# Gathering the small experts in pairs, and moving a transposition, in a two-layer decoder kernel

## The chip, the cores and the metric

One core of a Trainium2 chip runs the whole kernel in one launch. The metric is device time in microseconds (us): the median of three runs, 1362.1 us before the change (1359.48 to 1362.96). Lower is better. The profile is of a single execution of the same kernel.

## The reference

Two post-LayerNorm decoder layers on 256 tokens of width 1024, all in float32. Layer 0 mixes (pooling and window attention) and applies a dense SwiGLU; layer 1 mixes (dilated attention and a short convolution) and applies a SwiGLU of 8 experts, of which each token takes 2. The change lies in those experts, whose computation is, cut to its core:

```python
logits = xt @ w_router
top_logit, top_e = lax.top_k(logits, 2)
gates = jax.nn.softmax(top_logit, axis=-1)
# for each expert e, on the tokens that chose it:
y = (jax.nn.silu(xb @ w_gate[e]) * (xb @ w_up[e])) @ w_down[e]
# added back to each token, times its gate
x = layer_norm(ALPHA * x + out)
```

An expert's weights are 1024 x 3584 for gate and for up and 3584 x 1024 for down. All of them are read, whatever the routing.

## The kernel before

Weights come in pieces of 128 x 2048 float32 (1 MB), one DMA each in the expert stage, issued by SP in the order of use as soon as one of the raw buffers is free. A float32 product is made from rounded halves (fp32r): ScalarE casts a piece to its high half (`wh`, `hi()`, L258), VectorE subtracts that from the raw piece for the low half (`wl`, `lo()`, L275), and TensorE multiplies with both. Four wh and three wl buffers run in rings. Each time TensorE is done with a piece (`drop`), `pump` issues the next cast and, at most two pieces ahead, the next subtraction. A few pieces are "native": TensorE multiplies the raw float32 piece without a split.

Each engine works through its instructions in the order of the program, which is written out by hand (`manual_schedule`).

The experts are sorted by their number of tokens. If at least five of seven have 64 tokens or fewer, these five are "light" (1 to 5), the others (0, 6, 7) "heavy"; this is the branch that runs here. An expert has 7 chunks of 512 inner columns; a chunk is one call of `step`: gate (two pieces), up (two pieces), then the two down products of the chunk before it (`prev`), since its activations have to be turned in between. The order of chunks (`mixed`) interleaves light and heavy ones, mostly one heavy, two light.

- A heavy chunk has tokens in high and low halves, 128 columns each, and each product takes three matmuls (`mm3`, L316 to L318). Its down pieces are native in most of the run (L1224). ScalarE applies silu to the gate, VectorE multiplies with up (L1441), TensorE transposes the result (L1246).
- A light chunk packs high and low halves of up to 64 tokens as 128 columns, so two matmuls do (L1226, L1227). TensorE transposes gate (`fold_of` into `sg`, L1237), ScalarE copies one half of the result (L1240), VectorE adds the other (L1241, the sg sum), ScalarE applies silu (L1436). Up is copied out (L1439), transposed and summed the same way into `us`; the transposes and the copy stand between the two down products, the us sum and the product sg x us (L1466) behind both.

Before an expert starts, its tokens are gathered by matmuls with a one-hot matrix `oh` (VectorE, L1169): `half` (L1185) or `thin` (L1190), products in L1179, with the tokens' high and low halves `xkh` and `xkl` as separate fp32r products. These halves are made once, by `copy` and `tensor_sub` at L1089, L1091, L1115 and L1306. `part()`, called after gate and after up of every step, runs the next part of a gather that is queued; `part(p)` at the start of a step finishes that of p. `follow` queues the next gather. Light gathers go to the two halves of `places[1]`, heavy ones to `places[0]`.

Of the kernel before, what the change touches and what calls it, by code (L numbers as in the profile page):

```python
# [10 lines left out]
F32 = mybir.dt.float32  # L11
F32R = mybir.dt.float32r
# [8 lines left out]
KC = D // 128  # L21
# [66 lines left out]
def trunk(ctx, tc, stream, x_tok, x_t, pos, ln_w, ln_b, pool_bd, pool_sc, sinks, conv_w, router, cf, cb, windows,  # L88
# [798 lines left out]
    with tc.tile_pool(name="od1", bufs=1) as e1, tc.tile_pool(name="od2", bufs=2) as e2:  # L887
# [153 lines left out]
    raw3 = ctx.enter_context(tc.tile_pool(name="raw3", bufs=1))  # L1041
    xk, yb = [raw2.tile([128, PIECE], F32R, name=f"xk{i}") for i in range(2)], \
        raw2.tile([128, PIECE], F32R, name="yb")
    raws = [raw3.tile([128, PIECE], F32, name=f"raw{RAW1 + i}") for i in range(RAW2 + RAW3 - 3)]
# [3 lines left out]
    ctx.enter_context(tc.manual_schedule())  # L1048
    xkh, xkl = [t.rearrange("p (i d) -> p i d", i=2) for t in xk]
    lgp = bank()  # L1050
    lg0 = lgp[:, :2 * NE].rearrange("p (i e) -> p i e", e=NE)

    def route(norm, c):
# [10 lines left out]
        return logits  # L1064

    def split_tokens(i):
        split(xkh[:, i], xkl[:, i], x[:, i])

# [19 lines left out]
    lga = route(na, 4)  # L1088
    nc.scalar.copy(xkh[:, 0], x[:, 0])  # L1089
    lgb()  # L1090
    nc.vector.tensor_sub(xkl[:, 0], x[:, 0], xkh[:, 0].bitcast(F32))  # L1091
    lgb = route(na, 6)
# [21 lines left out]
    keep(KEEP[2])  # L1114
    nc.scalar.copy(xkh[:, 1], x[:, 1])  # L1115
    W.hi()
# [44 lines left out]
    class Unit:  # L1161
# [13 lines left out]

        def gather(self, a, c, b, m):
            for k in range(c, c + 512 // m):
                for i in range(2):
                    nc.tensor.matmul(b[:, (k - c) * m:(k - c + 1) * m],  # L1179
                                     (xkh, xkl)[a][:, i, k * 128:(k + 1) * 128],  # L1180
                                     self.oh[:, i], start=i == 0, stop=i == 1)

        def half(self, c, a, b, copy):
            self.gather(a, c, b, 128)
            copy(self.xg[a][:, c:c + 4], b.rearrange("p (k s) -> p k s", s=128))  # L1185

        def thin(self, a):
            b = bank()
            self.gather(a, 0, b, LIGHT)
            nc.scalar.copy(self.xg[0][:, :, a * LIGHT:(a + 1) * LIGHT], b.rearrange("p (k s) -> p k s", s=LIGHT))  # L1190

        def parts(self):
            yield self.start()
            for j in range(2 if self.light else 4):
                if self.light:
                    self.thin(j)
                else:
                    self.half(4 * (j % 2), j // 2, bank(), nc.vector.tensor_copy if j == 3 else nc.scalar.copy)
                yield

# [90 lines left out]
    m2 = ctx.enter_context(tc.tile_pool(name="mo2", bufs=1, side="right"))  # L1291
    rings.add("oh", [m2.tile([128, 2, 128], F32R, name="oh")])
    rings.add("ohb", [m2.tile([128, 2, 128], F32R, name="ohb")])
# [8 lines left out]
    rings.add("bank", [bank() for _ in range(4)])  # L1302
    places = [big_tile(t) for t in ("mh", "ml")]
    unit = Unit(places[0], 0, False, slot)
    unit.start()
    nc.vector.tensor_sub(xkl[:, 1], x[:, 1], xkh[:, 1].bitcast(F32))  # L1306
    W.lo()
    for c in (0, 4):
        unit.half(c, 0, acc(), nc.scalar.copy)
    for c in (0, 4):  # L1310
        unit.half(c, 1, bank(), nc.vector.tensor_copy if c == 0 else nc.scalar.copy)
    for _ in range(4):
# [6 lines left out]
    def gates():  # L1319
        nc.vector.tensor_scalar(gt[:, 0], gt[:, 1], 1.0, None, op0=OP.add)  # L1320
        nc.vector.reciprocal(gt[:, 0], gt[:, 0])
        nc.vector.tensor_mul(gt[:, 1], gt[:, 1], gt[:, 0])
        nc.vector.tensor_mul(gate, hots[0], bc(gt[:, 0]))
        nc.vector.tensor_mul(hots[1], hots[1], bc(gt[:, 1]))
        nc.vector.tensor_add(gate, gate, hots[1])
        nc.scalar.activation(x, x, AF.Copy, scale=ALPHA)

# [41 lines left out]
    class Experts:  # L1369
# [14 lines left out]
        def gather(self, p):  # L1384
            light = p in self.light
            half = KC * 128
            place = places[1][:, p % 2 * half:(p % 2 + 1) * half] if light else places[self.kind(p)]
            self.units[p] = Unit(place, p, light, slots)
            self.queue.append((p, self.units[p].parts()))

# [16 lines left out]
        def step(self, s):  # L1407
# [37 lines left out]
            if self.prev is not None:  # L1445
# [4 lines left out]
                W.drop()  # L1450
            if light:
                fold_up = fold_of(us, h)
            if left == 0:
                unit.back()
            if self.prev is not None:
                finish(down_half(self.y[pe], pht, 1, pn, W.take(None)))
                W.drop()
                if ended:
                    split_y(yb[:, :D], yb[:, D:], self.y.pop(pe))
                    ended.back()  # L1460
                    self.todo = combine_of(pe, ended.oht)
            if light:
                ht = rings.next("hh")
                s3 = sg.rearrange("p (k t) -> p k t", t=LIGHT)
# [20 lines left out]
        def follow(self, p, n):  # L1485
            if not self.light:
                after = p + 1 if n == 1 and p else None
            elif p in self.light:
                after = p + 1 if n == 0 and p + 1 in self.light else None
            else:  # L1490
                after = next((q for q in range(p + 1, NE) if q not in self.light), None) if n == NCH - 1 else None
# [15 lines left out]
    def tail(x8):  # L1507
# [4 lines left out]
        for _ in range(7):  # L1512
            nc.tensor.matmul(spare, xkh[:, 0, :128], xkh[:, 0, :512], start=True, stop=True)
        e, n, ht = x8.prev
# [207 lines left out]
```

## Time and profile before

| | |
|---|---|
| median of three runs | 1362.1 us |
| the profiled execution | 1365.56 us |
| its span, first to last instruction | 1363.8 us |
| TensorE busy | 1321.2 us, 97% |
| VectorE busy | 1084.4 us, 80% |
| ScalarE busy | 917.3 us, 67% |
| granted TensorE clock, mean | 0.990 |
| the page's row of DMA, mean of the span | 313 GB/s |

The expert stage runs from about 470 us to 1345 us. Times of rows are us from the first instruction. Engines are PE (TensorE; PEld its weight loads), DVE (VectorE), ACT (ScalarE) and SP. A row of a timeline is one group of instructions: start, time from the first start to the last end, engine, line, operation, written tile <- read tiles, shape, count; in brackets is the idle time of the engine just before and what ended it. Matmuls overlap, and their ends are modelled, so the distance of two starts says more than the length of a row. A native product shows as two records.

### The profile page before, as it was taken

To read this page: it belongs to the slowest core of one execution; us is meant where nothing else is said; L and a number is where in the kernel's file an instruction comes from. 1 tells how busy PE (TensorE), PEld (TensorE's weight loads), DVE (VectorE), ACT (ScalarE), POOL (GpSimd) and SP (SyncE) were. 2 spreads that over 40 slices of the span, in tenths; PEclk is the share of its full clock that TensorE was granted. 3 is DMA by queue.
4 is the path that set the end of the run, shared out by engine and by line. 5 is a ranking of instruction groups with operands and counts; after the bars stand their busy time and mean duration, and the time that the engine had idled before them with its cause. 6 is when DMAs were issued, how large, how long until landed. Compare 5 with 4: busy or idle time off the path is not lost. (4 is left out here: it accounts for less than half of the span.)

```text
span 1363.8 us, 18760 instructions
## 1 busy us (share of the span) xinstructions
PE 1321.2 (97%) x6944; PEld 1069.5 (78%) x6944; DVE 1084.4 (80%) x1110; ACT 917.3 (67%) x1026; POOL 2.5 (0%) x8
## 2 busy tenths in 40 slices
PE   8999999999999989999999999999999999999995
PEld 6888999988999778877777777787777877777764
DVE  6866555587655688899898899898889979988987
ACT  5735444455544477788776788778678769776883
POOL 0000000000000000000000000000000000000000
PEclk9999999999999999999999999999999999999998
DMA  8617655535424689999999999999999999999991
GB/s 261 234 62 222 205 187 186 187 124 186 155 78 149 261 307 370 346 417 401 420 387 362 377 420 420 418 419 419 419 392 419 419 405 419 420 419 350 418 411 41
DMA packets 72375, 426.61 MB, mean 313 GB/s; under 512 B 8914, under 2 KB 9682, under 8 KB 30548
## 3 DMA queue, kind: packets, MB, share of 16 engines
q1 hardware_dynamic: 71412, 424.32, 79.9%
q0 software_dynamic: 576, 0.62, 0.3%
q8 instruction: 56, 0.92, 0.3%
q10 hardware_dynamic: 288, 0.39, 0.1%
q14 instruction: 43, 0.35, 0.1%
HBM read 424.88 MB, written 1.05 MB: 312 GB/s over the span
## 5 line engine op out<-in xcount | busy, mean ns | idle before, releaser
L275 DVE TENSOR_TENSOR wl<-raw,wh 128x2048 fp32r<-128x2048 f32 (+2 forms) x435 | 823.6, 1914 | 155.6 <-ACT wh L258 126.9
L258 ACT CAST wh<-raw 128x2048 fp32r<-128x2048 f32 (+2 forms) x437 | 695.0, 1607 | 140.1 <-PE bank L318 62.8
L1226 PE MATMUL bank<-wh,ml 128*128 128x512 f32 x536 | 220.5, 411 | 1.1 <-ACT h L1427 1.1
L1227 PE MATMUL bank<-wl,ml 128*128 128x512 f32 x536 | 211.5, 395 | 0.9 <-DVE wl L275 0.6
L318 PE MATMUL bank<-wl,mh 128*128 128x512 f32 x336 | 131.8, 392 | 3.1 <-DVE wl L275 3.1
L316 PE MATMUL bank<-wh,mh 128*128 128x512 f32 x336 | 134.0, 399 | 0.0
L317 PE MATMUL bank<-wh,mh 128*128 128x512 f32 x336 | 131.4, 391 | 0.4 <-ACT mh L1185 0.4
L1227 PEld LDWEIGHTS bank<-wl,ml 128*128 128x128 f32 x536 | 100.8, 188 | 28.5 <-DVE wl L275 6.1
L1226 PEld LDWEIGHTS bank<-wh,ml 128*128 128x128 f32 x536 | 100.8, 188 | 22.6 <-issue 3.1
L316 PE MATMUL bank<-xth,wh 128*128 128x256 f32 x416 | 118.1, 284 | 0.0
L317 PE MATMUL bank<-xth,wl 128*128 128x256 f32 x416 | 117.7, 283 | 0.0
L318 PE MATMUL bank<-xtl,wh 128*128 128x256 f32 x416 | 117.7, 283 | 0.0
L1226 PE MATMUL acc<-wh,hh 128*128 128x512 f32 (+1 forms) x308 | 115.3, 381 | 0.8 <-DVE hh L1468 0.8
L1224 PE MATMUL acc<-raw,hf 128*128 128x512 f32 x256 | 115.2, 593 | 0.0
L1227 PE MATMUL acc<-wl,hh 128*128 128x512 f32 (+1 forms) x308 | 112.9, 373 | 0.0
L1224 PEld LDWEIGHTS acc<-raw,hf 128*128 128x128 f32 x256 | 47.1, 190 | 47.1 <-issue 46.0
L316 PEld LDWEIGHTS bank<-xth,wh 128*128 128x128 f32 x416 | 79.8, 192 | 0.4
L317 PEld LDWEIGHTS bank<-xth,wl 128*128 128x128 f32 x416 | 79.8, 192 | 0.4
L318 PEld LDWEIGHTS bank<-xtl,wh 128*128 128x128 f32 x416 | 79.8, 192 | 0.0
L318 PEld LDWEIGHTS bank<-wl,mh 128*128 128x128 f32 x336 | 63.5, 189 | 16.9 <-DVE wl L275 3.5
L317 PEld LDWEIGHTS bank<-wh,mh 128*128 128x128 f32 x336 | 63.5, 189 | 14.6 <-issue 1.0
L316 PEld LDWEIGHTS bank<-wh,mh 128*128 128x128 f32 x336 | 63.5, 189 | 13.8 <-issue 1.0
(284 smaller groups left out, 1849.0 us busy)
## 6 DMA issues: line engine op xcount, KB each, us to landing
raw<-in_stream SPq DMA_DIRECT2D x326, 1024.0 KB, 9.8
raw<-in_stream SPq DMA_DIRECT2D x142, 512.0 KB, 4.9
ln_wb<-in_ln_w SPq DMA_DIRECT2D x3, 512.0 KB, 8.1
ln_wb<-in_ln_b SPq DMA_DIRECT2D x3, 512.0 KB, 9.5
xraw<-in_x_t SPq DMA_DIRECT2D x4, 256.0 KB, 7.2
raw<-in_stream SPq DMA_DIRECT2D x4, 256.0 KB, 5.0
x<-in_x_tok SPq DMA_DIRECT2D x1, 1024.0 KB, 7.0
win<-in_windows SPq DMA_DIRECT2D x1, 768.0 KB, 10.9
```

Source lines behind the costliest of these rows:

```text
L258: nc.scalar.copy(self.split[k][0][:, c], self.raw[k][:, c])
L275: nc.vector.tensor_sub(wl[:, c], self.raw[k][:, c], wh[:, c].bitcast(F32))
L316: nc.tensor.matmul(o, ah, bh, start=start, stop=False)
L317: nc.tensor.matmul(o, al, bh, start=False, stop=False)
L318: nc.tensor.matmul(o, ah, bl, start=False, stop=stop)
L1224: nc.tensor.matmul(o, a if a.dtype == F32 else a.bitcast(F32), bh, start=start, stop=stop)
L1226: nc.tensor.matmul(o, a, bh, start=start, stop=False)
L1227: nc.tensor.matmul(o, a, bl, start=False, stop=stop)
```

## The change

The tokens are no longer split ahead of the gather: `xk` and its copies and subtractions go. The gather multiplies the raw float32 tokens with a float32 one-hot, natively, once in place of two fp32r products, and the result is split as it leaves the accumulator, by a ScalarE cast and a VectorE subtraction.

Light experts are gathered two at a time, (1, 2), (3, 4) and 5 alone: their one-hots stand side by side in `oh`, one native product of 128 columns serves both, and four casts and four subtractions of 256 elements split the result. The pairs go to `places[1]` and to a third place in the memory that `xk` had; (3, 4) is queued behind the fourth chunk of expert 1, and 5 behind the fourth chunk of 3, where each light expert's gather was queued behind the first chunk of the one before. `x` after the scaling by ALPHA becomes a tile of its own, `xsum`.

In a light chunk the transposes of up and ScalarE's copy of them (`fold_of(us, h)`) move from between the two down products to behind both, and so behind the casts and subtractions that the second `drop` issues.

```diff
-    xk, yb = [raw2.tile([128, PIECE], F32R, name=f"xk{i}") for i in range(2)], \
-        raw2.tile([128, PIECE], F32R, name="yb")
+    xsum = raw2.tile([128, 2, D], F32, name="xsum")
+    yb = raw2.tile([128, PIECE], F32R, name="yb")
+    third = raw2.tile([128, PIECE], F32R, name="xg2")
...
-    nc.scalar.copy(xkh[:, 0], x[:, 0])
...
-    nc.vector.tensor_sub(xkl[:, 0], x[:, 0], xkh[:, 0].bitcast(F32))
...
-    nc.scalar.copy(xkh[:, 1], x[:, 1])
...
-        def gather(self, a, c, b, m):
-            for k in range(c, c + 512 // m):
+        def gather(self, c, b):
+            m = LIGHT if self.light else 128
+            for k in range(512 // m):
                 for i in range(2):
-                    nc.tensor.matmul(b[:, (k - c) * m:(k - c + 1) * m],
-                                     (xkh, xkl)[a][:, i, k * 128:(k + 1) * 128],
+                    nc.tensor.matmul(b[:, k * m:(k + 1) * m], tokens[:, i, (c + k) * 128:(c + k + 1) * 128],
                                      self.oh[:, i], start=i == 0, stop=i == 1)
...
+            hi, lo = [t[:, c:c + 512 // m] for t in self.xg] if not self.light else \
+                     [self.xg[0][:, :, a * m:(a + 1) * m] for a in range(2)]
+            split(hi, lo, b.rearrange("p (k s) -> p k s", s=m))
+
+        def parts(self, other=None):
+            if other is not None:
+                oh = rings.tiles["oh"][0]
+                self.oh, other.oh = [oh[:, :, e * LIGHT:(e + 1) * LIGHT] for e in range(2)]
+                other.start()
             yield self.start()
-            for j in range(2 if self.light else 4):
-                if self.light:
-                    self.thin(j)
-                else:
-                    self.half(4 * (j % 2), j // 2, bank(), nc.vector.tensor_copy if j == 3 else nc.scalar.copy)
-                yield
+            if other is not None:
+                for c in (0, 4):
+                    b = bank()
+                    for k in range(4):
+                        for i in range(2):
+                            nc.tensor.matmul(b[:, k * 128:(k + 1) * 128],
+                                             tokens[:, i, (c + k) * 128:(c + k + 1) * 128], oh[:, i],
+                                             start=i == 0, stop=i == 1)
+                    b = b.rearrange("p (k s) -> p k s", s=128)
+                    for e, u in enumerate((self, other)):
+                        x2 = u.xg[0][:, c:c + 4]
+                        split(x2[:, :, :LIGHT], x2[:, :, LIGHT:], b[:, :, e * LIGHT:(e + 1) * LIGHT])
+                    yield
+                return
+            for c in (0,) if self.light else (0, 4):
+                yield self.gather(c, bank())
...
-    rings.add("oh", [m2.tile([128, 2, 128], F32R, name="oh")])
+    rings.add("oh", [m2.tile([128, 2, 128], F32, name="oh")])
...
-    places = [big_tile(t) for t in ("mh", "ml")]
+    places = [big_tile(t) for t in ("mh", "ml")] + [third]
+    tokens, x = x, xsum
     unit = Unit(places[0], 0, False, slot)
     unit.start()
-    nc.vector.tensor_sub(xkl[:, 1], x[:, 1], xkh[:, 1].bitcast(F32))
     W.lo()
     for c in (0, 4):
-        unit.half(c, 0, acc(), nc.scalar.copy)
-    for c in (0, 4):
-        unit.half(c, 1, bank(), nc.vector.tensor_copy if c == 0 else nc.scalar.copy)
+        unit.gather(c, bank())
...
-        nc.scalar.activation(x, x, AF.Copy, scale=ALPHA)
+        nc.scalar.activation(x, tokens, AF.Copy, scale=ALPHA)
...
+                ps = [q for q in (p, p + 1) if q in self.light]
+                place = places[1 + (p - 1) // 2 % 2]
...
-            if light:
-                fold_up = fold_of(us, h)
             if left == 0:
                 unit.back()
...
             if light:
+                fold_up = fold_of(us, h)
                 ht = rings.next("hh")
...
-                after = p + 1 if n == 0 and p + 1 in self.light else None
+                after = p + 2 if n == 3 and p % 2 and p + 2 in self.light else None
```

## Rows read from the trace of the kernel before

**Rows 1.** The page's busy times, shares of the span and instruction counts of each engine.

```profile
PE 1321.2 (97%) x6944; PEld 1069.5 (78%) x6944; DVE 1084.4 (80%) x1110; ACT 917.3 (67%) x1026; POOL 2.5 (0%) x8
```

**Rows 2.** Windows A:B: length; busy PE, PEld, DVE, ACT, POOL; clock, DMA share, GB/s.

```profile
564.00:628.20 64.20, 61.81 (x300) 49.88 (x298) 63.11 (x42) 54.28 (x48) 0.00 (x0) 1.00 0.99 398
...
636.00:670.98 34.98, 34.60 (x157) 27.48 (x155) 34.77 (x26) 28.55 (x24) 0.00 (x0) 1.00 1.01 418
...
727.10:760.20 33.10, 33.10 (x155) 25.35 (x154) 25.40 (x18) 23.23 (x20) 0.00 (x0) 1.00 0.95 388
...
767.42:802.00 34.58, 34.51 (x157) 27.49 (x155) 34.37 (x23) 28.54 (x24) 0.00 (x0) 1.00 1.01 421
...
1010.28:1044.88 34.60, 34.53 (x157) 27.49 (x155) 34.38 (x23) 28.56 (x24) 0.00 (x0) 1.00 1.01 421
...
1173.63:1208.22 34.59, 34.52 (x157) 27.49 (x155) 34.37 (x23) 28.55 (x24) 0.00 (x0) 1.00 1.01 419
```

**Rows 3.** Waits of ScalarE, 560 to 1250: total us, times, longest us.

```profile
ACT wh L258 <- PE bank L317: 4.4, 5, 1.2
...
ACT wh L258 <- ACT wh L258: 4.2, 5, 1.0
...
ACT wh L258 <- issue: 2.4, 2, 1.3
```

**Rows 4.** Timeline of one cycle: start, us, instruction, count [idle before, releaser].

```profile
1003.09 0.42 DVE L1241 TENSOR_TENSOR sg<-sg,bank 128x256 f32<-128x256 f32 x1 [0.61 <-ACT sg L1240]
...
1004.33 3.59 PE L1224 MATMUL acc<-raw,hf 128*128 128x512 f32 x8
...
1005.79 4.58 DVE L275 TENSOR_TENSOR wl<-raw,wh 128x2048 fp32r<-128x2048 f32 x2 [2.27 <-ACT wh L258]
...
1007.76 0.60 PE L1237 MATMUL bank<-cst,h 128*128 128x128 f32 x4
...
1010.28 0.41 DVE L1241 TENSOR_TENSOR us<-us,bank 128x256 f32<-128x256 f32 x1
...
1011.23 0.80 PE L1226 MATMUL bank<-wh,ml 128*128 128x512 f32 x1
...
1023.78 0.39 PE L316 MATMUL bank<-wh,mh 128*128 128x512 f32 x1
...
1025.46 0.41 DVE L1241 TENSOR_TENSOR us<-us,bank 128x256 f32<-128x256 f32 x1
...
1053.63 0.80 PE L1226 MATMUL bank<-wh,ml 128*128 128x512 f32 x1
```

**Rows 5.** Timeline of TensorE: gathers at 470 and 908, native products at 411.

```profile
470.54 2.10 PE L1179 MATMUL acc<-oh,xk 128*128 128x128 f32 x16 [0.69 <-PE bank L1151]
...
472.48 1.95 PE L1179 MATMUL bank<-oh,xk 128*128 128x128 f32 x16
...
908.92 1.87 PE L1179 MATMUL bank<-oh,xk 128*128 128x64 f32 x16
...
411.03 0.78 PE L1013 MATMUL bank<-v,pt 128*128 128x64 f32 x6
```

**Rows 6.** Timeline of VectorE: a split, a pair of one-hots, an sg sum.

```profile
487.51 0.69 DVE L129 TENSOR_TENSOR hl<-bank,hh 128x512 fp32r<-128x512 f32 x1 [1.37 <-ACT hh L128]
...
905.99 0.41 DVE L1169 TENSOR_SCALAR oh<-iota,hot 128x64 fp32r<-128x64 bf16 x2
...
923.55 0.42 DVE L1241 TENSOR_TENSOR sg<-sg,bank 128x256 f32<-128x256 f32 x1 [2.04 <-ACT sg L1240]
```

**Rows 7.** Timeline of a chunk of expert 5: transposes of up and the us sum.

```profile
1292.91 0.60 PE L1237 MATMUL bank<-cst,h 128*128 128x128 f32 x4
...
1293.95 0.42 DVE L1241 TENSOR_TENSOR us<-us,bank 128x256 f32<-128x256 f32 x1 [0.32 <-ACT us L1240]
```

**Rows 8.** Waits of TensorE, 560 to 1250: total us, times, longest us.

```profile
PE bank L1237 <- ACT h L1439: 2.3, 4, 1.4
...
PE bank L1179 <- ACT h L1439: 2.1, 1, 2.1
```

More of the change, by code (lines that the diff above doesn't have):

```diff
@@ L1048, in trunk @@
     ctx.enter_context(tc.manual_schedule())
-    xkh, xkl = [t.rearrange("p (i d) -> p i d", i=2) for t in xk]
     lgp = bank()
@@ L1064, in route @@
         return logits
-    def split_tokens(i):
-        split(xkh[:, i], xkl[:, i], x[:, i])
     na.add(1, oa[1])
@@ L1181, in gather @@
                                      self.oh[:, i], start=i == 0, stop=i == 1)
[L1183 to L1192, printed above, removed]
-            yield self.start()
-            for j in range(2 if self.light else 4):
-                if self.light:
-                    self.thin(j)
-                else:
-                    self.half(4 * (j % 2), j // 2, bank(), nc.vector.tensor_copy if j == 3 else nc.scalar.copy)
-                yield
+            hi, lo = [t[:, c:c + 512 // m] for t in self.xg] if not self.light else \
+                     [self.xg[0][:, :, a * m:(a + 1) * m] for a in range(2)]
@@ L1384, in gather @@
         def gather(self, p):
[L1385 to L1389, printed above, removed]
+            half, ps = KC * 128, [p]
+            if p in self.light:
+                ps = [q for q in (p, p + 1) if q in self.light]
+                place = places[1 + (p - 1) // 2 % 2]
+                for j, q in enumerate(ps):
+                    self.units[q] = Unit(place[:, j * half:(j + 1) * half], q, True, slots)
+            else:
+                self.units[p] = Unit(places[self.kind(p)], p, False, slots)
+            self.queue.append((p, self.units[p].parts(*[self.units[q] for q in ps[1:]])))
         def part(self, until=None):
@@ L1512, in tail @@
         for _ in range(7):
-            nc.tensor.matmul(spare, xkh[:, 0, :128], xkh[:, 0, :512], start=True, stop=True)
+            nc.tensor.matmul(spare, places[1][:, :128], places[1][:, :512], start=True, stop=True)
         e, n, ht = x8.prev
```

## The prediction

> **What bounds the kernel now.** I read four views in order: the page's busy times, the waits of ScalarE in the expert stage, windows over single cycles of that stage, and the timeline of one cycle. The page says TensorE: 97% busy, against 80% for VectorE [rows 1]. The end of a matmul is modelled, so this share does not say how near TensorE is to its peak. In the expert stage the DMA engines show a share of 1.01 [rows 2], yet the first reader of a piece, ScalarE's wh cast (L258), is never held up by a transfer: its waits name TensorE, itself or issue [rows 3]. Landed weights lie ready; the transfers are full but ahead.
>
> The stage repeats a cycle: a heavy chunk (12 fp32r matmuls a piece, native down products), then two light chunks (8 a piece). In the window 1010.28 to 1044.88, the part of a cycle that follows the us sum of the first light chunk, VectorE is busy 34.38 of 34.60 us [rows 2]. Seven such windows (one starts at 636.00, the plain six run from 767.42 to 1173.63) show the same. VectorE idles only at two places, both in the first light chunk: 0.6 us ahead of the sg sum and 2.27 us ahead of the next wl subtraction, which waits for ScalarE's cast [rows 4]. After that it works without a break until the weights of the next such chunk are split, and TensorE meets its own last wl there. So TensorE and VectorE are both full, and the cycle of 42.40 us (next gate at 1011.23 to next gate at 1053.63 [rows 4]) has no slack for VectorE. That decides what follows: work taken from TensorE pays only where VectorE idles, and any wait put into VectorE's queue lengthens the cycle.
>
> **The products of the gather.** A thin gather now takes 16 fp32r products of 64 columns in 1.87 us [rows 5], two of them per small expert. A wide one takes 16 products of 128 columns from 470.54 to 472.48, 121 ns each, and 1.95 us for the next 16 [rows 5]: the width makes no difference, each product pays about 112 ns. A native product of 128 columns is not in the trace. The nearest row is L1013, native on 64 columns: three products leave six records in 0.78 us, about 0.1 us a record, two records a product [rows 5]. The far end is L1224, native on 512 columns: eight records in the 3.43 us from 1004.33 to 1007.76, 429 ns a record [rows 4]. Between 0.1 and 0.43 us a record I take 0.11, since the weight load is the same 128 columns as in L1179; a product is then 0.22 us and 16 are 3.6 us. So a heavy gather stays at 3.6 us (32 x 0.112 against 16 x 0.22), the single small expert 5 too, and each pair saves 3.6 us of TensorE, 7.2 us in all.
>
> The Trainium skill (FP8 and Floating Point Precision, TensorE Precision Notes) says that true fp32 takes four passes through the array. The trace shows two records a product here; by four passes at 0.11 us the pairs would save nothing and every other gather would cost 3.6 us more, which is the fourth rival below.
>
> **What the splits cost.** Where ScalarE alone copied a thin gather, VectorE now subtracts too: 0.41 us for a subtraction of 256 elements (the us sum is as large [rows 4]), 0.69 us for one of 512 [rows 6], and it stands in VectorE's queue waiting for TensorE's gather and ScalarE's cast, as it waited 1.37 us for such a cast at 487.51 [rows 6]. Behind it are the wl subtractions and behind those TensorE.
>
> **The moved transposition.** In the first light chunk after a heavy one, TensorE transposes up at 1007.76, between the native downs, and VectorE starts the us sum at 1010.28, as soon as its own queue lets it, while the second down product runs until the next gate at 1011.23 or, without overlap, 1011.6 [rows 4]. After the change the four transposes begin when the second down is done, at 1007.76 + 3.43 = 1011.2. From transposes to us sum it takes 1.04 us when nothing else is in the way (1292.91 to 1293.95, where VectorE waited 0.32 us for the copy [rows 7]). So the sum starts at 1012.2 and VectorE stands still for 1.96 us. Queued behind it are the gating product and the wl subtractions of the whole cycle, without a gap to swallow the wait; TensorE then waits for wl at the end. Price: 2.0 us a cycle, at most 2.3 if ScalarE's casts, also later by as much, fall behind too; not below zero, since nothing is taken from VectorE. TensorE's gain, the waits of the transposes for ScalarE's copy of up (2.3 us in all [rows 8]), lies mostly in cycles that VectorE sets. In the second light chunk the move is free: VectorE reaches the us sum at 1025.46, after the transposes would be done: the next gate starts at 1023.78 [rows 4], and 1.04 us on is 1024.8. Where a heavy chunk follows the first light one, VectorE has idle time in the heavy chunk, and the wait is hidden.
>
> **The sum**, place by place:
> - Six plain cycles (windows 767.42 to 1173.63): 6 x 2.0 = +12.0.
> - The cycle at 636 to 681 now takes the pair (3, 4): 2.0 for the move, four one-hots at 0.2 [rows 6] and four subtractions at 0.42, VectorE being busy 34.77 of 34.98 [rows 2]: +4.5 (3.6 to 5.4).
> - 727 to 760: expert 3's gather goes. VectorE is busy only 25.40 of 33.10 us [rows 2], so TensorE's 3.6 us are gained whole: -3.6.
> - 882 to 921 (and 1053 to 1092, the same pattern): the gathers of 4 and 5 go. VectorE gains a pair of one-hots, 0.41, and loses 2.0 to the move; its idle 2.04 us ahead of the next sg sum [rows 6] shrinks and hides 1.4 of that. Net +0.2 each, 0 taken; TensorE's 3.6 us are eaten.
> - 976 to 1002: expert 5's gather arrives, and its subtraction holds VectorE until TensorE has gathered: +3.6.
> - 564 to 628, where expert 2's gather goes: VectorE is busy 63.11 of 64.20 [rows 2]: only its one-hots are gained, -0.4.
> - 681 to 727: heavy expert 6 gathers in two parts, not four; the wait of 2.1 us for a bank [rows 8] goes, while VectorE waits once more: -1.0 (-2.5 to +1).
> - The first gather: VectorE subtracts twice where it copied once, and the wl subtractions behind it, for which the first gate products wait, come later by one subtraction of 512 elements, 0.69 [rows 6]: +0.7. The four casts and subtractions of the tokens (about 1.1 us each) that go lie where VectorE and ScalarE wait anyway: 0. The scaling by ALPHA only changes its target: 0.
> - The chunks of expert 5 alone at the end: the wait of 1 to 2 us falls into VectorE's idle time there (the 0.32 us at 1293.95 [rows 7] is some of it): 0.
>
> Together +15.8, say +16. No weight DMA is moved or added: SP issues one when a raw buffer comes free, so the queue only runs later by what VectorE loses; POOL is not touched. The profiled execution took 1365.56 us (span 1363.8), which gives 1381.6; it lay 3.5 us above the median of 1362.1, and against the median the forecast is 1378. Its own range, from the bounds above and 2.3 a cycle: 1370 to 1387.
>
> **The rivals.**
> 1. TensorE bounds the stage, as the page's 97% says [rows 1]. Then the 7.2 us of the pairs and the 2.3 us of waits at the transposes come off whole: 1352.6. It decides if a wait of 2 us in VectorE's queue after the first light chunk is made up within the cycle, so that TensorE never sees it. For it: TensorE waits little. Against it: 34.38 of 34.60 us, seven times. Chance 0.13.
> 2. The wait is hidden after all (ScalarE's casts come earlier into the 2.27 us gap, say). Then the sum lacks 14: 1364 or, with the 1.6 us that each of the two cycles with gathers then gives back, 1361. Chance 0.12.
> 3. The transfers bound the stage; share 1.01 speaks for it, the casts that never wait for one against it [rows 2, 3]. Then nothing moves while compute stays ahead: 1362. The Trainium skill (SBUF — State Buffer, A bandwidth-pool intuition) holds that HBM is almost always the end-to-end bottleneck; the waits here disagree. Chance 0.03.
> 4. A native product costs twice what I take (four records): heavy gathers and expert 5's add 4 x 3.6, the pairs gain nothing: about 1392. Chance 0.05.
> That the pairs are not formed at all: L1190 shows light gathers in this run, and the pair path hangs on the same list; no chance of its own.
>
> **How the numbers follow.** The forecast keeps 0.67. A measurement of this kernel can tell about 0.3%, 4.1 us, from no change: faster means below 1358, slower above 1366.2. Faster: rival 1, 0.13. Within: rivals 2 and 3 but for a rest, 0.13. Slower: the forecast, rival 4 and that rest, 0.74. The range leaves out rival 1 and the most of rival 4: 1358 to 1388.
>
> **What would show it.** In the profile after, VectorE's us sum after a native down should carry an idle time of about 2 us with ScalarE's us copy as its releaser, and the plain cycle should take 44.4 us for 42.4. The gather's records should number 32 a pair at 0.11 us. The stretch that held expert 3's gather should be 3.6 us shorter, the ones that held those of 4 and 5 no shorter. If the cycle stays at 42.4 with the idle time there, VectorE had slack that I did not see; if the idle time is missing, the us copy did not wait for the second down; if native products take 0.4 us, rival 4 holds.

## The result and the profile after

The changed kernel takes 1374.98 us (median of 4 runs, 1372.91 to 1376.51), the kernel before 1362.19 us beside it: a ratio of 1.0093, with a 95% interval of 1.0074 to 1.0111. That is 12.8 us slower; the forecast was 1378. The profiled execution has a span of 1374.6 us for 1363.8, so 10.8 us more.

The page's busy times (busy us, share of the span, instructions of each engine) answer [rows 1]:

```profile
PE 1324.0 (96%) x6880; PEld 1059.8 (77%) x6880; DVE 1085.0 (79%) x1120; ACT 907.8 (66%) x1020; POOL 2.5 (0%) x8
```

TensorE has 64 records fewer and VectorE ten operations more; TensorE is busy 2.8 us longer, VectorE 0.6. The rest of the 10.8 us is standing time, and the waits of VectorE between 560 and 1260 say where (total us, times, longest):

```profile
DVE wl L275 <- ACT wh L258: 28.8, 14, 2.3
DVE us L1243 <- ACT us L1242: 24.1, 13, 1.9
DVE sg L1243 <- ACT sg L1242: 8.8, 14, 0.9
```

The list of the kernel before begins:

```profile
DVE wl L275 <- ACT wh L258: 37.8, 22, 2.3
DVE sg L1241 <- ACT sg L1240: 14.2, 15, 3.2
DVE yb L129 <- ACT yb L128: 7.6, 8, 2.8
```

The line of the us sum is new: 13 times it stands for ScalarE's copy of up. The lines of wl and sg became shorter through the gathers alone; with the transposition put back (g_only, below) they stand at the same 28.8 and 8.8. One cycle in the timeline, the one that answers [rows 4] (start, us, instruction, count, [idle before, releaser]):

```profile
1008.90 0.42 DVE L1243 TENSOR_TENSOR sg<-sg,bank 128x256 f32<-128x256 f32 x1 [0.61 <-ACT sg L1242]
...
1010.14 7.03 PE L1226 MATMUL acc<-raw,hf 128*128 128x512 f32 x16
...
1011.60 4.58 DVE L275 TENSOR_TENSOR wl<-raw,wh 128x2048 fp32r<-128x2048 f32 x2 [2.28 <-ACT wh L258]
...
1017.00 0.60 PE L1239 MATMUL bank<-cst,h 128*128 128x128 f32 x4
1017.64 0.37 ACT L1242 COPY us<-bank 128x256 f32<-128x256 f32 x1 [2.00 <-PE bank L1239]
1018.05 0.42 DVE L1243 TENSOR_TENSOR us<-us,bank 128x256 f32<-128x256 f32 x1 [1.88 <-ACT us L1242]
...
1017.36 0.48 PE L1228 MATMUL bank<-wh,xg 128*128 128x512 f32 x1
...
1061.51 0.48 PE L1228 MATMUL bank<-wh,xg 128*128 128x512 f32 x1
```

The two native halves now run in one piece (16 records), the transposes follow at 1017.00, ScalarE's copy at 1017.64, and the us sum at 1018.05, with 1.88 us of idle time ahead of it. The gaps at the sg sum (0.61) and at wl (2.28) are what they were in [rows 4]: the wait came on top. From next gate (1017.36) to next gate (1061.51) the cycle takes 44.15 us for 42.40.

The stretch of the cycle that follows the us sum (length; busy PE, PEld, DVE, ACT, POOL; clock, DMA share, GB/s) answers the sixth line of [rows 2]:

```profile
1018.05:1052.40 34.35, 33.32 (x152) 26.16 (x150) 34.20 (x22) 27.90 (x23) 0.00 (x0) 1.00 1.01 420
```

VectorE works 34.20 of 34.35 us there, for 34.38 of 34.60 before; TensorE now only 33.32, where it was at 34.53 of 34.60.

**Where the time went.** The moment at which ScalarE starts to read the gate (the copy in a light chunk, the silu in a heavy one) tells, chunk by chunk, how far a trace is behind that of the kernel before. The view of one line (engine, operation, count: shortest/median/longest ns, first and last start us) gives the first and last light chunk, and, in a window of three copies, the first plain cycle. Of the kernel before:

```profile
L1427 ACT COPY h<-bank x35: 573/587/590, 566.8 to 1330.5; 128x512 f32<-128x512 f32 x35
...
L1427 ACT COPY h<-bank x3: 587/587/587, 772.7 to 815.1; 128x512 f32<-128x512 f32 x3
```

Of the changed kernel:

```profile
L1431 ACT COPY h<-bank x35: 568/586/589, 567.0 to 1341.2; 128x512 f32<-128x512 f32 x35
...
L1431 ACT COPY h<-bank x3: 573/575/589, 772.1 to 816.2; 128x512 f32<-128x512 f32 x3
```

The first plain cycle is 44.1 for 42.4, the 35 chunks together take 10.7 us more (the rows print tenths; the table below is worked out from the same starts to the hundredth). It gives the change of each stretch against the kernel before, stretches named by the times of the kernel before, for the main runs of the next section:

| stretch, us | after | f_only | g_only | g_placed | defer | heavy_two | what lies in it |
|---|---|---|---|---|---|---|---|
| 567 to 626 | -1.3 | -0.2 | -1.1 | -1.1 | -0.9 | 0.0 | expert 2's gather gone |
| 626 to 687 | +6.2 | +1.5 | +4.8 | +0.9 | +5.5 | +0.9 | pair (3, 4) |
| 687 to 741 | -3.5 | -0.1 | -3.5 | -3.5 | -3.9 | -3.5 | heavy expert 6's gather |
| 741 to 773 | -2.1 | +1.5 | -3.6 | +0.3 | -3.6 | 0.0 | expert 3's gather gone |
| 773 to 872 | +2.0 | +1.9 | 0.0 | +0.1 | +0.4 | 0.0 | cycles without a gather |
| 872 to 936 | +1.5 | +3.2 | -1.7 | -1.7 | -1.8 | 0.0 | expert 4's gather gone |
| 936 to 986 | -0.5 | -0.2 | -0.7 | -0.7 | -0.1 | +0.5 | heavy expert 7's gather |
| 986 to 1016 | +5.0 | +1.5 | +3.5 | 0.0 | +3.1 | 0.0 | expert 5's gather arrives |
| 1016 to 1058 | +1.7 | +1.7 | 0.0 | 0.0 | +0.6 | 0.0 | a plain cycle |
| 1058 to 1121 | -1.6 | +0.2 | -1.7 | -0.2 | -2.1 | 0.0 | expert 5's old gather gone |
| 1121 to 1237 | +3.5 | +3.5 | 0.0 | 0.0 | +0.4 | 0.0 | cycles without a gather |
| 1237 to 1330 | -0.2 | -0.2 | -0.1 | -0.1 | -0.2 | -0.1 | expert 5 alone |
| sum | +10.7 | +14.5 | -4.2 | -6.0 | -2.7 | -2.1 | |

What a run does before 567 is not compared: there the executions differ by up to 6 us in kernels whose work up to that point is the same.

### The profile page after: what moved, and what is told of

Read it like the earlier page. It is cut to its first block, busy times and chain, and to the rows that moved or that the text cites. A ratio compares the mean times of both kernels' runs of the same rounds, so it can differ in the third digit from the quotient of the medians.

```text
span 1374.6 us, 18609 instructions
## 1 busy us (share of the span) xinstructions
PE 1324.0 (96%) x6880; PEld 1059.8 (77%) x6880; DVE 1085.0 (79%) x1120; ACT 907.8 (66%) x1020; POOL 2.5 (0%) x8
## 4 chain that ended last, share of the span: by engine, by line
PE 75%; DVE 15%; ACT 4%; issue 4%; DMA 1%; SPq 0%; DVEq 0%; ACTq 0%
DVE wl L275 9%; PE bank L318 9%; PE bank L317 9%; PE bank L316 9%; PE acc L1226 8%; PE bank L1229 6%; PE bank L1228 5%; PE acc L318 4%; PE acc L317 4%; PE acc L316 4%; PE acc L1229 3%; PE acc L1228 3%; ACT wh L258 2%; PE bank L1239 2%; DMA raw<-in_stream 1%
## 5 line engine op out<-in xcount | busy, mean ns | idle before, releaser
L1228 PE MATMUL bank<-wh,ml 128*128 128x512 f32 x312 | 128.0, 410 | 0.0
L1229 PE MATMUL bank<-wl,ml 128*128 128x512 f32 x312 | 124.4, 399 | 2.9 <-DVE wl L275 2.1
L1229 PE MATMUL acc<-wl,hh 128*128 128x512 f32 (+1 forms) x308 | 113.7, 377 | 4.4 <-DVE wl L275 4.0
L1228 PE MATMUL acc<-wh,hh 128*128 128x512 f32 (+1 forms) x308 | 113.0, 373 | 1.5 <-DVE hh L1471 1.5
L1226 PE MATMUL acc<-raw,hf 128*128 128x512 f32 x256 | 112.4, 592 | 0.0
L1229 PE MATMUL bank<-wl,xg 128*128 128x512 f32 x224 | 90.0, 402 | 3.4 <-DVE wl L275 2.3
L1228 PE MATMUL bank<-wh,xg 128*128 128x512 f32 x224 | 90.2, 403 | 0.0
L1229 PEld LDWEIGHTS bank<-wl,ml 128*128 128x128 f32 x312 | 58.7, 188 | 21.5 <-DVE wl L275 9.3
L1229 PEld LDWEIGHTS acc<-wl,hh 128*128 128x128 f32 x308 | 57.9, 188 | 21.2 <-DVE wl L275 11.0
## 6 DMA issues: line engine op xcount, KB each, us to landing
win<-in_windows SPq DMA_DIRECT2D x1, 768.0 KB, 10.7
```

What stands on the lines that cost most here:

```text
L1226: nc.tensor.matmul(o, a if a.dtype == F32 else a.bitcast(F32), bh, start=start, stop=stop)
L1228: nc.tensor.matmul(o, a, bh, start=start, stop=False)
L1229: nc.tensor.matmul(o, a, bl, start=False, stop=stop)
```

## The experiments

**The two halves of the change.** f_only is the kernel before with this alone (and nothing at the old place):

```
             if light:
+                fold_up = fold_of(us, h)
                 ht = rings.next("hh")
```

> The kernel before with the moved transposition alone; the gathers stay as they were. Theory (VectorE stands still for the transposes and has no slack): the six plain cycles lengthen by 1.74 us each, as they did in the changed kernel (42.40 to 44.14), the one at 636 to 681 by as much, the two that hold a gather by 0.6 to 2.0 each: 13.4 to 16.2 us in all, so 1375.5 to 1378.5 for 1362.2. Rival A (the loss comes from the gathers, the move is hidden): 1361 to 1364. Rival B (TensorE bounds, and the 2.3 us that its transposes waited for ScalarE come back): 1360.

It took 1379.57 us, a ratio of 1.0119 (1.0093 to 1.0146).

```profile
L1427 ACT COPY h<-bank x35: 568/586/595, 565.7 to 1343.8; 128x512 f32<-128x512 f32 x35
...
L1427 ACT COPY h<-bank x3: 568/578/588, 774.3 to 818.4; 128x512 f32<-128x512 f32 x3
```

The move alone costs 14.5 us in the 35 chunks, more than the whole change, and the first plain cycle is again 44.1 us long. (The 14.5 lie in the range expected; the median lies 1.1 us above it.) The shifts come in steps of 1.5 to 1.7 us at nine places, each time where two light chunks follow a heavy one with native down products (just ahead of the cycles that begin at 641, 773, 815, 888, 936, 1016, 1058, 1136 and 1179). Where a heavy chunk follows the first light one, they come to 0.25 us or less. Two more places have two light chunks behind a heavy one and no step, at 687 and 1256. An expert ends there, and VectorE has the splits of y ahead of the us sum, which then waits for nothing:

```profile
681.97 0.69 DVE L129 TENSOR_TENSOR yb<-acc,yb 128x512 fp32r<-128x512 f32 x1 [1.39 <-ACT yb L128]
682.58 0.41 DVE L1241 TENSOR_TENSOR us<-us,bank 128x256 f32<-128x256 f32 x1
```

Rivals A and B fall.

g_only is the changed kernel with the transposition back between the two downs.

> The changed kernel with the transposition of up put back between the two down products: the gathers alone. Theory: what is left of the places of the sum (expert 3's gather gone -3.6, expert 5's arriving +3.2, the pair at 636 to 681 +4.3, the heavy gather in two parts at 681 to 735 -3.6, the rest about -1) is -1 to -3 us: 1359 to 1361 for 1362.2. Rival (TensorE bounds the stage, so that the 7.2 us of the pairs and the heavy gather's waits come off whole): 1353 to 1355. Rival (the gathers hold the loss): above 1366.

```profile
L1431 ACT COPY h<-bank x35: 567/587/591, 562.2 to 1321.6; 128x512 f32<-128x512 f32 x35
```

It took 1358.20 us, 0.9966 (0.9951 to 0.9981): the gathers alone gain, 3.8 us by the medians, 4.2 in the 35 chunks, a little more than the 1 to 3 expected and less than TensorE's 7.2. Place by place the two columns add up to the changed kernel within 0.4 us, 14.5 - 4.2 = 10.3 for 10.7. Neither half needs the other.

**Is it the wait, or the later transposes?** defer leaves TensorE's order as the change has it, and issues what reads the transposes one weight piece later (abridged, the comments are added here):

```
+                def join():
+                    fold_up()            # ScalarE's copy and the us sum
+                    nc.vector.tensor_mul(sg, sg, us)
+                    nc.scalar.copy(ht[:, :, :LIGHT], s3)
+                self.late = [join, lambda: nc.vector.tensor_sub(...)]   # one after each gate half
```

> The changed kernel with its transposes of up where the change puts them, behind both down products, but with ScalarE's us copy, VectorE's us sum, the gating product and its cast issued only behind the cast and the subtraction of one more weight piece, after the next chunk's first gate products. Theory (the price is VectorE's stand of 1.9 us, not the place of the transposes on TensorE): the us sum no longer waits, the plain cycle is back at 42.4 us, and of the 12.8 us all but the gathers' share goes: 1359 to 1364. Rival (the later transposes themselves, or ScalarE's lateness, cost the time): 1371 to 1376.

It took 1358.54 us, 0.9971 (0.9958 to 0.9985), half a microsecond below the range expected. The row of the gate copies, and the waits of VectorE in the same window as above:

```profile
L1433 ACT COPY h<-bank x35: 571/587/589, 561.0 to 1321.9; 128x512 f32<-128x512 f32 x35
...
DVE wl L275 <- ACT wh L258: 28.7, 14, 2.3
DVE sg L1245 <- ACT sg L1244: 8.8, 14, 0.9
DVE mh L129 <- ACT mh L128: 8.6, 3, 3.4
```

The line of the us sum is gone, the other two stand, and the 35 chunks take 2.7 us less than before, where the changed kernel's took 10.7 more, with the transposes still behind both downs. Of the 14.9 us that lie between the changed kernel and g_only, 13.4 are gone and 1.5 are left. So the stand in the queue is nearly the whole price, not the place on TensorE. defer takes the wait out of ScalarE's queue as well (2.00 us ahead of its copy at 1017.64); that this wait was not the price shows in the window above, where VectorE, at 34.20 of 34.35 us, hardly waits for a late cast behind the us sum.

**Who is full, and by how much?** Three runs add or take away work at the steps with native down products; the transposition stays where it was. pe_minus leaves out one native product of four in each half:

```
                 start, stop = n == 0 and c == 0, n == NCH - 1 and c == 3
+                if pl is None and c == 1:
+                    continue
```

> The kernel before with one of the four native products of every native down half left out (that part of the down products is missing): TensorE has two products of two records less in each of 16 steps, 4 x 0.43 = 1.72 us each; the work of VectorE and ScalarE is untouched. Theory (VectorE sets the nine cycles in which two light chunks follow a heavy one): those nine stay at their length (42.4 us, 0.3 less at most), the other seven gain up to 1.72: 1350 to 1360. Rival (TensorE sets them): 16 x 1.72 = 27.5 us less, 1335.

```profile
L1429 ACT COPY h<-bank x35: 565/586/594, 564.8 to 1315.1; 128x512 f32<-128x512 f32 x35
...
L1429 ACT COPY h<-bank x3: 575/584/587, 766.7 to 808.9; 128x512 f32<-128x512 f32 x3
```

1349.93 us, 0.9903 (0.9885 to 0.9922). The first plain cycle is 42.2 us for 42.4: of 1.72 us taken from TensorE 0.20 come back there, 0.24 in the cycle from 1016 to 1058, and between 0 and 0.3 in all nine, while the other seven steps give 1.55 to 1.71 each; all 16 come to 13.4. VectorE sets the nine cycles as soon as TensorE is about 0.24 us shorter.

pe_plus does the reverse, eight fp32r products between the transposes of up and the second down:

```
+                for _ in range(8):
+                    nc.tensor.matmul(spare, xkh[:, 0][:, :128], xkh[:, 0][:, :512], start=True, stop=True)
```

> The kernel before with eight more fp32r products of 512 columns (0.228 us each, 1.82 us together, into a bank that nobody reads) on TensorE in the 16 steps with native down products, behind the transposes of up and ahead of the second native down; VectorE and ScalarE do what they did. Theory as it stands after the other runs (TensorE's own cycle is 42.4 us, VectorE's 0.24 to 0.3 shorter): every one of the 16 steps lengthens by about 1.8 us, 29 us in all, so about 1390. Rival (VectorE alone sets the nine cycles and TensorE has room in them, as the prediction had it): the nine lengthen by 1.3 at most and more likely by nothing, the other seven by 1.8: 1375 or less.

```profile
L1427 ACT COPY h<-bank x35: 567/588/592, 564.3 to 1357.5; 128x512 f32<-128x512 f32 x35
...
L1427 ACT COPY h<-bank x3: 588/588/590, 777.6 to 821.9; 128x512 f32<-128x512 f32 x3
```

1392.72 us, 1.0209 (1.0179 to 1.0240): 29.6 us in the 35 chunks, about 1.85 in each of 16 steps, the nine among them. TensorE has no room in them either.

dve_plus puts four additions of 256 elements behind the us sum:

```
                 fold_up()
+                    for _ in range(4):
+                        nc.vector.tensor_add(pad, pad, pad)
                 nc.vector.tensor_mul(sg, sg, us)
```

> The kernel before with four more VectorE additions of 256 elements (0.42 us each, 1.68 us together, on a tile of their own) between the us sum and the gating product of every step with native down products, 16 steps in all; nothing waits for a transposition. Theory (VectorE has no slack in the nine cycles with two light chunks and has it in the other seven): nine times 1.4 to 1.68, so +12.6 to +15: 1375 to 1377. Rival A (VectorE's 2.27 us gap ahead of the wl subtraction takes it up): 1362 to 1365. Rival B (no slack anywhere): +27, 1389.

```profile
L1429 ACT COPY h<-bank x35: 567/586/592, 565.0 to 1349.3; 128x512 f32<-128x512 f32 x35
...
L1429 ACT COPY h<-bank x3: 567/577/590, 776.5 to 820.2; 128x512 f32<-128x512 f32 x3
...
1022.14 1.80 DVE L1470 TENSOR_TENSOR pad<-pad 128x256 f32<-128x256 f32 x4
```

1384.06 us, 1.0158 (1.0133 to 1.0183): 20.7 us in the 35 chunks, more than expected. The nine cycles gave 1.4 each, 12.7 together, as the theory has it: with the four additions (last row) the gating product starts 2.05 us behind the us sum (1021.81 and 1023.86) where it was 0.45 (1010.28 and 1010.73), which is 1.6 us, and 0.24 of slack come off. The other 8 us fell at four places that I had not counted: one more step with a heavy chunk ahead of a light one, at 583 (1.6; there were 17 such steps, not 16), and the ends of experts (687, 986 and 1256; 1.6, 3.2 and 1.6), where the splits of y and the combine load VectorE. Why one of them costs 3.2 us, more than was added, was not tried. Rival A falls: the 2.27 us gap takes up nothing of work that stands behind it.

**The heavy gather.** heavy_two is the kernel before with its fp32r halves handed out two at a time:

```
                     self.half(4 * (j % 2), j // 2, bank(), ...)
+                    if j % 2 == 0:
+                        continue
                 yield
```

> The kernel before, fp32r gathers and transposition as they were, but a heavy gather is handed out in two parts of two halves, not in four parts. Theory (the 3.5 us won at 687 to 709 come from the two-part form: the last parts no longer queue for a bank behind ScalarE's copy of up, 2.1 us): 2 to 4 us less, 1358 to 1360. Rival (the native products and VectorE's share of the split won them): 1361 to 1363.

By the medians, where 2 to 4 us less were expected, it can't be told from no change (1364.25 us, 1.0007, 0.9991 to 1.0023). The trace tells more: between 687 and 741 it is 3.5 us shorter, as in the changed kernel, and it loses 0.9 just ahead of that, as g_placed does, where no pair is gathered: 2.6 net. In the waits of TensorE the line with 2.1 us of [rows 8] has become

```profile
PE bank L1179 <- ACT h L1429: 1.1, 1, 1.1
```

and the other stretches stand at 0.0 but for the second heavy gather's +0.5. So the gain there is that of the two-part form; native products and VectorE's part of the split changed nothing there.

**A better place.** g_placed is g_only with

```
-                after = p + 2 if n == 3 and p % 2 and p + 2 in self.light else None
+                after = p + 1 if n == 0 and p % 2 == 0 and p + 1 in self.light else None
```

> As the kernel with the gathers alone, but the pair (3, 4) is gathered after the first chunk of expert 2, in the stretch at 727 to 760 where VectorE is busy 25.40 of 33.10 us, and expert 5 after the first chunk of expert 4, as in the kernel before. Theory (a gather costs nothing where VectorE idles and its whole VectorE work where it doesn't): against the gathers alone the pair's 4.3 us at 636 to 681 and the 3.2 us at 976 to 1002 go, the 3.6 us of expert 3's gather come back, so 3 to 4 us less: 1356 to 1357. Rival (the 3.6 us won at 681 to 735 were only the pair's lateness caught up there, and go with it): 1360 to 1361.

It took 1356.65 us, 0.9955 (0.9938 to 0.9973), the lowest median of those that compute everything, and faster than both kernels. By the table 3.9 of the 4.8 us at 626 to 687 go (the other 0.9 is the heavy gather's) and expert 5's 3.5; 3.9 at expert 3's place and 1.5 at expert 5's are lost again: -6.0 for -4.2. The 3.5 us at 687 to 741 stayed, so the rival falls.

**Can VectorE be kept ahead?** best adds to defer and the better places a lead of the splits that leaves native pieces out of the count.

> The changed kernel with the deferred us sum, the pair (3, 4) and expert 5 gathered in the stretches of the earlier run, and the lead of the weight splits counted in pieces that are split (a native piece takes no place in it), so that ScalarE and VectorE go on splitting during the native down products, where VectorE had its gap of 2.27 us. Theory (VectorE sets the nine cycles; with this gap filled TensorE does, about 0.5 us shorter by its own products): 9 x 0.5 less than the 1356.7 of the gathers placed alone, 1350 to 1354. Rival (the gap only moves, since the split buffers are full): 1356 to 1358.

It took 1357.93 us, 0.9959 (0.9944 to 0.9974), so nothing beyond g_placed. The wl waits for ScalarE (28.7 us in defer) left the list, and this took their place:

```profile
DVE us L1248 <- ACT us L1247: 33.4, 13, 2.9
```

The rival holds in its number: the wait only moved. That the split buffers are full during the native downs, so that VectorE has to stand somewhere, is the likely reason and is not shown by this run. Two more runs gave it buffers in exchange for raw ones (and the transposition between the downs): wide4 a fourth wl, wide45 also a fifth wh.

> The kernel with the gathers placed and the transposition between the downs, the lead counted in split pieces, and one raw buffer turned into a fourth wl buffer, so that VectorE may be one subtraction (2.28 us) further ahead when the native down products begin. Theory (VectorE stands there because its buffers are full, and has to make it up afterwards): the nine cycles lose what VectorE sets, down to TensorE's own products, 0.5 us or more each: 1350 to 1353. Rival A (the gap only moves to another wait, as with the lead counted alone): 1356 to 1358. Rival B (one raw buffer less, and the casts begin to wait for transfers, the DMA share being at 1.01): above 1360.

> As the run with a fourth wl buffer, and a fifth wh buffer from a second raw buffer, so that ScalarE's casts may lead too. Theory: the subtractions of the fourth buffer no longer wait for their casts (2.27 us in a cycle before): 1348 to 1352. Rival A (the fourth wl buffer already took what there was): equal to that run within 2 us. Rival B (two raw buffers less, the casts wait for transfers): above 1360.

wide4 took 1465.39 us, 1.0744 (1.0715 to 1.0773). No side had expected this much; rival B had only "above 1360", and its reason fails, for in the list of ScalarE's waits no cast waits for a transfer (two subtractions do, for 3.5 us). The waits of VectorE and, below, of ScalarE in it, 560 to 1260:

```profile
DVE wl L279 <- ACT wh L262: 130.1, 72, 2.3
```

```profile
ACT sg L1446 <- DVE sg L1249: 82.9, 27, 4.6
ACT hh L1477 <- DVE sg L1476: 58.0, 25, 3.3
```

The two engines wait for each other in turn. The likely reason, not tried by itself, is that with the same limit on both leads each subtraction is issued right behind the cast of its own piece. wide45, where casts may lead again, took 1362.51 us, 1.0000 (0.9982 to 1.0018). Its waits of VectorE and of ScalarE:

```profile
DVE us L1250 <- ACT us L1249: 22.1, 13, 1.9
```

```profile
ACT wh L262 <- DMA raw<-in_stream: 10.9, 12, 4.1
```

The theory's 1348 to 1352 was missed, and rival B came in its number and its sign: the casts now wait for transfers, which they never did in [rows 3]; 6.5 of the 10.9 us come after 1121, and from 1121 to 1237 this run loses 5.7 us against the kernel before. (The Trainium skill, SBUF — State Buffer, A bandwidth-pool intuition, has HBM as almost always the end-to-end bottleneck; in the kernel before no cast waits for a transfer, and that they wait with two raw buffers less doesn't show the memory itself to be the limit.) In the first plain cycle, well ahead of that, the timeline and the view of the line have

```profile
760.53 0.42 DVE L1250 TENSOR_TENSOR us<-us,bank 128x256 f32<-128x256 f32 x1 [1.67 <-ACT us L1249]
...
L1438 ACT COPY h<-bank x3: 587/587/596, 767.3 to 809.8; 128x512 f32<-128x512 f32 x3
```

VectorE stands 1.67 us ahead of the us sum, and the cycle takes 42.5 us as before: where VectorE has been given a lead, such a wait costs nothing, and TensorE's own work sets the cycle, as pe_plus suggests.

## Why the prediction was right, and where it was not

**The wait itself** came as worked out. Set against the start of the native halves, the transposes were due at +6.87 us (1011.2 against 1004.33) and came at +6.86; the us sum was due at +7.9 and came at +7.91; the idle time was to be 1.96 and is 1.88.

**Its price** is the term that was mis-sized most. It was put at 2.0 us, on the step that the cycle has no slack for VectorE. It has 0.24: pe_minus shortens the cycle by that much and no more. Then 1.88 - 0.24 = 1.64, and f_only's nine places mean 14.5 / 9 = 1.61. The slack stands in [rows 2]: 34.60 - 34.38 = 0.22 us of the window, which was read as none. By the next gates the plain cycles grew by 1.74 in the changed kernel, once by 1.30 (with the second heavy gather in it); the six came to 10.0 for 12.0.

**Which places pay** was right: the six plain cycles, the one of the pair, and the two that hold the gathers of 4 and 5; none where a heavy chunk follows the first light one.

**Both engines full.** The prediction took TensorE and VectorE both to be full, so that a wait in VectorE's queue lengthens the cycle and work taken from TensorE pays only where VectorE idles. pe_minus, pe_plus and dve_plus bear this out, with the two equal within 0.24 us in the plain cycles. (The expectation of pe_plus gives the prediction as having room on TensorE; it had not.) Rival 1 was right that TensorE is full (pe_plus, 1.85 a step) and wrong that this makes room: f_only and pe_minus show that shortening it gains only to the point where VectorE takes over.

**The gathers of 4 and 5** were put at 2.0 for the move, -0.41 for the one-hots and -1.4 for VectorE's idle gap ahead of the next sg sum, +0.2 net. Both halves came: f_only pays 1.5 and 1.7 there, and g_only gives back 1.7 at each. But it is not the wait that falls into the gap. In f_only the gap stands at 2.04 us as in [rows 6]; with the gather gone it shrinks, in g_only and in the changed kernel alike (the sg sum of [rows 6] in g_only, then in the changed kernel):

```profile
913.70 0.42 DVE L1243 TENSOR_TENSOR sg<-sg,bank 128x256 f32<-128x256 f32 x1 [0.62 <-ACT sg L1242]
...
924.87 0.42 DVE L1243 TENSOR_TENSOR sg<-sg,bank 128x256 f32<-128x256 f32 x1 [0.62 <-ACT sg L1242]
```

That is 1.42 us, with the one-hots 1.8, close to the 1.7 given back: here TensorE's saving reaches VectorE, because VectorE stood there for transposes that TensorE reached only behind the gather.

**The pair at 636 to 681** was put at 4.5 us and measured 5.4, when the 0.9 of the heavy gather is taken off the 6.2: 1.5 for the move (2.0 predicted) and 3.9 for the gather (2.5 predicted). Missing were VectorE's waits for ScalarE's casts of the gather, in the timeline of the changed kernel

```profile
648.77 0.42 DVE L129 TENSOR_TENSOR xg<-bank,xg 128x256 fp32r<-128x256 f32 x1 [0.83 <-ACT xg L128]
649.63 0.42 DVE L129 TENSOR_TENSOR xg<-bank,xg 128x256 fp32r<-128x256 f32 x1 [0.44 <-ACT xg L128]
...
660.96 0.42 DVE L129 TENSOR_TENSOR xg<-bank,xg 128x256 fp32r<-128x256 f32 x1 [0.44 <-ACT xg L128]
```

which is 1.7 us; with them VectorE's part is 4.2, and 0.24 of slack come off. I had weighed this wait with the row of 1.37 in [rows 6], and then left it out of the sum.

**The heavy gather** was put at -1.0 (-2.5 to +1) and gave -3.5 + 0.9 = -2.6, just outside its bounds. The bank wait of 2.1 us went as said; the counterweight, VectorE's added wait, cost nothing, for heavy_two, which lacks it, is no faster there. The second heavy gather (936 to 986, -0.7) was not in the sum at all, and expert 2's (-1.1 for -0.4) was too small.

**Right as put**: expert 3's gather gone, -3.6 (g_only -3.6); expert 5's arriving, +3.6 (+3.5). The start of the stage, +0.7, can't be read: from the first product of the first gather to the first light gate the changed kernel takes 96.5 us and the kernel before 96.3, but f_only, with the same instructions there as the kernel before, 99.5. The native product's price holds, two records each (timeline of TensorE in the changed kernel):

```profile
644.74 1.95 PE L1191 MATMUL bank<-oh,x 128*128 128x128 f32 x16
657.42 1.95 PE L1191 MATMUL bank<-oh,x 128*128 128x128 f32 x16
```

These are 32 records a pair. Each row runs to the end of its last record; from start to start a record takes 0.11 us, as taken, and so does an fp32r product of [rows 5] in the kernel before. Rival 4 falls, and with it the count of four passes from the Trainium skill (FP8 and Floating Point Precision, TensorE Precision Notes) as a measure of time for products this narrow. At 512 columns it comes near: two records of 0.43 us [rows 4], where fp32r products follow each other every 0.23 us (L1228 and L1229 behind 1017.64 in the changed kernel).

So the total of 15.8 us, worked out, against 10.8 in the profiled executions was too high nearly everywhere. The six plain cycles account for 2.0 of the difference, the first heavy gather for 1.6, the second for 0.5 to 0.7 and expert 2's for 0.9; the pair, 0.9 too low, hides some of it. The bounds given place by place add up to about 1376 to 1383 around the forecast, not to the 1370 to 1387 called its own range; the measured 1374.98 lies just outside the former. That the medians are within 3 us of the forecast is in part luck: 2.1 of their 12.8 us do not lie in the 35 chunks, and the part ahead of these varies by more than that. It is not luck that the sign and the place came out, for the largest term, the waits, was the best founded.

## What to carry over

Before work is moved behind a long instruction on one engine, follow the first reader on the next engine: what is queued behind it pays the wait in full, less the slack that the windows show in that stretch, and idle time elsewhere in the cycle gives nothing back. Where two engines are within a few tenths of each other, a saving on the fuller one alone is worth only the difference (pe_minus), added work on it costs its whole length (pe_plus), and on the other its length less the difference (dve_plus). A gather or another job to be placed belongs where an engine that it needs has idle time: moving it there (g_placed) took off another 1.8 us in the chunks, on top of the 4.2 of the gathers alone.

## What was not expected of the hardware

The expert stage repeats almost to the hundredth: heavy_two and the kernel before, two executions of two programs, agree within 0.05 us in eight of the twelve stretches of the table. The part ahead of it does not: the first light gate was copied between 561.0 and 567.7 us in the profiled executions of the runs in the table, with the same instructions there in several of them. A change of 2 us in the stage, as heavy_two's, is thus lost in the medians and plain in the trace.

What the first part's length goes with is TensorE's granted clock. Of the 26 executions of the kernel before beside f_only, the six with a mean clock of 0.988 or less took 1365.6 to 1367.1 us, the four with 0.993 or more 1358.8 to 1360.6. The windows show where (changed kernel, then defer, whose first gates come at 567.0 and 561.0 with the same work up to there):

```profile
320.00:360.00 40.00, 36.68 (x216) 32.32 (x214) 26.15 (x50) 21.27 (x38) 0.00 (x0) 0.91 0.51 165
...
320.00:360.00 40.00, 37.28 (x247) 33.13 (x245) 28.69 (x50) 24.59 (x45) 0.00 (x0) 1.00 0.55 179
```

In windows of 40 us up to 560 the changed kernel has four below 1.00 (0.91 and three of 0.96), that is, partly at the lower of the clock's two levels, 1.2 for 2.4 GHz; defer has one (0.96); from 560 on the clock is 1.00 in both. That the clock is the cause, and what makes it fall there in one execution and not in another, was not tried.
